# Three of the five sums of an entry's tile, formed over transposed blocks in PSUM instead of over rows in SBUF

## The chip, the cores and the metric

The kernel runs on one core of a Trainium2 chip. The metric is the device time in microseconds (us) of one execution, as the median over several runs. A profile of one execution gives the span (from the first instruction to the last), what each engine did, and what ended each wait. The engines are TensorE (PE, with its weight loads as PEld), VectorE (DVE), ScalarE (ACT) and GpSimd (POOL); SyncE (SP) issues nearly all of the transfers.

## The reference

A decoder block over 1024 tokens of width 1024, in fp32: a half-step FFN, a mixer of two branches with gates, a second half-step FFN and a last norm. What matters here is only its outline:

```python
def rms_norm(x, g):
    y = x * lax.rsqrt(jnp.mean(x * x, axis=-1, keepdims=True) + RMS_EPS)
    return y * g

def swiglu(x, w1, w3, w2):
    return (jax.nn.silu(x @ w1) * (x @ w3)) @ w2

h = x
h = h + 0.5 * swiglu(rms_norm(h, ffn1_norm), w1a, w3a, w2a)      # 1024 -> 2816 -> 1024
u = rms_norm(h, mix_norm)
proj = u @ w_in                        # 1024 -> 2304 (q, k, v) + 512 (pool) + 2048 (gates)
...                                    # dilated attention, multi-scale pooling
h = h + (sigmoid(gA) * yA + sigmoid(gB) * yB) @ w_out
h = h + 0.5 * swiglu(rms_norm(h, ffn2_norm), w1b, w3b, w2b)
out = rms_norm(h, final_norm)
```

So there are three places where normed rows enter a large product: the first FFN, the mixer's input projection and the second FFN. The document calls them the three *entries*.

## The kernel before, in words

**Products.** Each large product is done by blocks of a 2 x 2 split with seven products of half size instead of eight (`Sevens`, `Quad`). The right factor is the normed activation, transposed, so that its model columns lie on the partitions. Of its four blocks b11, b12, b21, b22 (first index: lower or upper half of the 1024 columns, `LOWS` and `HIGHS`; second index: lower or upper half of the 1024 tokens) seven right factors are formed:

- product 1: b11; product 2: b21; product 3: b22,
- product 5: t1 = b12 - b11; product 6: t2 = b22 - t1; product 4: t4 = t2 - b21; product 7: t3 = b22 - b12.

Each block is 512 columns by 512 tokens, and is held as a high and a low part (fp32r), because each step of a product takes three TensorE matmuls: high by high, high by low and low by high (L314). One call of `product` gives 128 output columns for 512 tokens: four steps of 128 in depth, three matmuls each, so 12 matmuls of 128 x 128 weights by 512 tokens. Products 1 and 2 add into one bank, and so do 5 and 3. A `Quad` holds the seven products of one group of columns, a `Pair` two such groups a and b (`u_f10a`, `u_f10b` in the profile: first FFN, pair 0).

**Left factors.** `Quad.operand(m)` forms the left factor of product m from weight blocks, with one sum on DVE for products 7 and 4 (L351 for 7) and two for product 6 (L345, L347), then `Sevens.split`: a copy to the high part on ACT (L303), and the difference as the low part (L306) on POOL, or on DVE for every third factor of a stage. Inside an entry `Entry.operand` names POOL for it. The factor tiles are `wc`, the block sums `s`.

**Rows to blocks.** The tokens come in eight tiles of 128 rows, t = 0 to 3 (the lower half) and t = 4 to 7 (the upper half). A tile is scaled by its norm on DVE (L267 for a whole row). `Rows` (L381 to L385) then makes a block's 128 tokens out of a row: four PE transposes of 128 x 128 into one bank of PSUM (L381), an ACT copy of the bank to the high part (L382), and, when `lower` is called, the low part by DVE (L385).

**An entry.** The lower tiles give b11 and b21, which are transposed ahead of the loop. The loop in `Entry.run` (L406 to L440) takes the upper tiles t = 4 to 7, with two products of other pairs per tile (i, and k = i + 1; all of them products 1 or 2, which need b11 and b21 alone) to keep PE busy while the sums and transposes of that tile are made. In a tile the order before is: product i; the transposes of b22; the sums t1, t2, t4 over rows on DVE (L423, L424, L425) and t3 over rows on POOL (L426); the lower of b22; the operand for i + 2; `out(i)`, which takes the finished product from PSUM; product k; the operand for k + 2; the transposes of t1, t2, t4, t3, sixteen of them; the scaling of the next row (`high(t + 1, 1)`, L267); four lowers on DVE; `out(k)`; `after(t)`, which squares a later row on ACT. t1 and t3 take the place of the lower tile's blocks in `h[t - 4]`, t2 and t4 a half tile `s` each. b12 itself is no factor of any product, so it is never transposed. `more` (L790) issues the operands of the first pair's products 6 and 7 as soon as tile 6 and tile 7 are through. These two, M6 and M7 below, are the first products behind the loop.

**Order.** Around the entries the order of the instructions on each engine is the order in which the program issues them (`tc.manual_schedule()`); each engine works its own queue in that order and waits at the head of it. Waits between engines follow from the tiles that they share: SBUF tiles by pool and tag, PSUM by whole banks (tag "acc" or "mm", a few banks each). Two operations on one bank from two engines are put one behind the other.

The first FFN's entry is written out in `begin_up1` (L792 to L893), with `rows(t, what, c)` scaling half a row and transposing it; the mixer's lower tiles are done by `rows_first` (L1232) inside the last steps of the first FFN's down product; those of the second FFN by `rows_first2` and `lower` (L1874 to L1882) beside the output projection.

## Time and profile before

| | |
|---|---|
| runs | 1957.8, 1959.87 and 1957.8 us; median 1957.8 us |
| profiled execution, span | 1955.6 us, 25018 instructions |
| PE busy | 1914.1 us, 98% of the span |
| DVE busy | 1343.5 us, 69% |
| ACT busy | 759.4 us, 39% |
| POOL busy | 741.1 us, 38% |
| mean granted TensorE clock | 0.994 |
| DMA | 333.57 MB, 171 GB/s mean |
| PE's largest groups | L706 (down products), three groups of 616 matmuls with 240.0 to 240.9 us each |

How to read it: a share of busy time is an average over all stages, so the entries have to be read by their own stretches: 28.16 to 59.78 us, 666.37 to 697.60 us and 1297.20 to 1328.90 us for the loops over the upper tiles, about 31 us each, 94.6 us in all. In rows of single instructions the first column is the start in us from the span's beginning, the second the time that the instruction (or the run of xN alike) took, then engine, line, operation, output<-inputs, sizes and type; brackets give the idle time before it and who ended it. A PE row "128*128 128x512" is a matmul with 128 x 128 weights and 512 columns.

### The profile page before, as it was taken

How to read it: one execution, taken by the hardware profiler on the slowest of the kernel's cores; microseconds unless marked ns; L12 is line 12 of the kernel's file. 1: busy time of each engine (PE TensorE's matmuls, PEld its weight loads, DVE VectorE, ACT ScalarE, POOL GpSimd, SP SyncE). 2: the span in 40 equal slices, each digit the busy share in tenths (PEclk: the TensorE clock that was granted, in tenths of full speed). 3: DMA queues.
4: the chain of work that ended last, by engine and by line, in shares of the span. 5: the costliest groups of instructions: out<-in, count | busy, mean ns of one | idle time of the engine just before them, and what ended most of it. 6: DMA issues, size and time to landing. Idle time of an engine off the chain costs nothing. (4 is left out here: it accounts for less than half of the span.)

```text
span 1955.6 us, 25018 instructions
## 1 busy us (share of the span) xinstructions
PE 1914.1 (98%) x8938; PEld 1579.7 (81%) x8938; DVE 1343.5 (69%) x2012; ACT 759.4 (39%) x1361; POOL 741.1 (38%) x557
## 2 busy tenths in 40 slices
PE   9999999999999999999998999999999999999997
PEld 7788888888888887888876878887788888878885
DVE  7776556557686876568774886887665556577766
ACT  6333333334344533334344662253333333333343
POOL 5333333332222444445454365543333333322231
PEclk9999999999999999999998999999999999999999
DMA  4155223336465546765658887643523223454653
GB/s 185 44 194 169 85 86 117 121 124 208 156 246 201 167 120 230 232 220 185 232 218 289 241 241 261 253 161 96 190 102 135 82 87 120 139 204 135 212 195 142
DMA packets 147005, 333.57 MB, mean 171 GB/s; under 512 B 20160, under 2 KB 40896, under 8 KB 145344
## 3 DMA queue, kind: packets, MB, share of 16 engines
q1 hardware_dynamic: 138096, 308.00, 45.9%
q10 hardware_dynamic: 8784, 23.96, 3.5%
q8 instruction: 71, 1.16, 0.2%
q14 instruction: 54, 0.44, 0.1%
HBM read 229.61 MB, written 102.30 MB: 170 GB/s over the span
## 5 line engine op out<-in xcount | busy, mean ns | idle before, releaser
L706 PE MATMUL d_f<-bhi_f,alo_f 128*128 128x512 f32 x616 | 240.8, 391 | 2.4 <-POOL alo_f L668 2.2
L706 PE MATMUL d_f<-bhi_f,ahi_f 128*128 128x512 f32 x616 | 240.9, 391 | 0.2 <-ACT ahi_f L664 0.2
L706 PE MATMUL d_f<-blo_f,ahi_f 128*128 128x512 f32 x616 | 240.0, 390 | 0.0
L668 POOL TENSOR_TENSOR alo_f<-g_f,ahi_f 128x512 fp32r<-128x512 f32 x70 | 99.2, 1434 | 298.5 <-ACT ahi_f L664 289.8
L314 PE MATMUL u_mixm<-xhi_t_mix,wc_mixm 128*128 128x512 f32 x608 | 196.0, 393 | 2.7 <-POOL wc_mixm L306 2.3
L314 PE MATMUL u_mixm<-xhi_b_mix,wc_mixm 128*128 128x512 f32 x456 | 149.3, 393 | 2.0 <-DVE y_m L982 2.0
L706 PEld LDWEIGHTS d_f<-bhi_f,alo_f 128*128 128x128 f32 x616 | 115.7, 188 | 29.0 <-POOL alo_f L668 4.0
L314 PEld LDWEIGHTS u_mixm<-xhi_t_mix,wc_mixm 128*128 128x128 f32 x608 | 113.8, 188 | 29.0 <-POOL wc_mixm L306 4.9
L706 PEld LDWEIGHTS d_f<-bhi_f,ahi_f 128*128 128x128 f32 x616 | 115.8, 188 | 24.1 <-ACT ahi_f L664 0.6
L706 PEld LDWEIGHTS d_f<-blo_f,ahi_f 128*128 128x128 f32 x616 | 115.8, 188 | 23.8
L314 PE MATMUL u_mixm<-xlo_t_mix,wc_mixm 128*128 128x512 f32 x304 | 118.6, 390 | 0.0
L306 POOL TENSOR_TENSOR wc_mixm<-s_mixm,wc_mixm 128x512 fp32r<-128x512 f32 x52 | 75.8, 1459 | 99.7 <-ACT wc_mixm L303 84.0
L314 PEld LDWEIGHTS u_mixm<-xhi_b_mix,wc_mixm 128*128 128x128 f32 x456 | 85.7, 188 | 20.7 <-ACT late_hi L1125 2.8
L303 ACT ACTIVATE wc_mixm<-s_mixm 128x512 fp32r<-128x512 f32 x76 | 47.6, 629 | 122.8 <-DVE s_mixm L347 52.1
L314 PE MATMUL u_mixm<-xlo_b_mix,wc_mixm 128*128 128x512 f32 x228 | 88.9, 390 | 0.0
L664 ACT ACTIVATE ahi_f<-g_f 128x1024 fp32r<-128x1024 f32 x84 | 81.8, 974 | 2.0 <-DMA g_f<-gs_f 2.0
L306 POOL TENSOR_TENSOR wc_mixm<-raw,wc_mixm 128x512 fp32r<-128x512 f32 x40 | 60.4, 1515 | 44.9 <-ACT wc_mixm L303 42.0
L664 ACT ACTIVATE bhi_f<-s_f2w 128x512 fp32r<-128x512 f32 x55 | 32.8, 627 | 97.1 <-DVE s_f2w L684 86.8
L1854 PE MATMUL wo<-w_o,o_hi 128*128 128x512 f32 x224 | 69.3, 391 | 0.0
L314 PEld LDWEIGHTS u_mixm<-xlo_t_mix,wc_mixm 128*128 128x128 f32 x304 | 57.2, 188 | 11.7 <-DVE xlo_t_mix L385 0.2
L664 ACT ACTIVATE bhi_f<-s_f1w 128x512 fp32r<-128x512 f32 x55 | 32.9, 630 | 85.1 <-DVE s_f1w L684 80.2
L1616 PE MATMUL yp<-pool_in,wab 128*128 128x512 f32 x192 | 55.7, 426 | 4.2 <-DMA pool_in<-pool 4.2
(1300 smaller groups left out, 5099.8 us busy)
## 6 DMA issues: line engine op xcount, KB each, us to landing
g_f<-gs_f SPq DMA_DIRECT2D x70, 512.0 KB, 4.5
gs_f<-y_f SPq DMA_DIRECT2D x88, 256.0 KB, 2.3
raw<-in_w2a_dram SPq DMA_DIRECT2D x35, 512.0 KB, 4.1
raw<-in_w2b_dram SPq DMA_DIRECT2D x35, 512.0 KB, 4.0
gs_f<-gb_f SPq DMA_DIRECT2D x46, 256.0 KB, 2.3
raw<-in_w1a_dram SPq DMA_DIRECT2D x22, 512.0 KB, 4.6
raw<-in_w3a_dram SPq DMA_DIRECT2D x22, 512.0 KB, 6.3
raw<-in_w1b_dram SPq DMA_DIRECT2D x22, 512.0 KB, 4.5
```

The source lines that it names most:

```text
L303: ac.activation(w[:, 0], src, AF.Copy)
L306: eng.tensor_tensor(w[:, 1], src, w[:, 0].bitcast(F32), op=OP.subtract)
L314: pe.matmul(p, a, b, start=(start and k == 0 and q == 0), stop=(k == 3 and q == 2), skip_group_check=not start)
L664: ac.activation(hi[:, c], src, AF.Copy)
L668: eng.tensor_tensor(lo[:, d], src[:, o], hi[:, d].bitcast(F32), op=OP.subtract)
L706: pe.matmul(self.banks[m][t], l, r, start=(first and q == 0), stop=(last and q == 2))
L1616: pe.matmul(p, a, b, start=(j == 0), stop=(j == 11))
L1854: pe.matmul(banks[m][t], l, r, start=(st == 0 and j == 0 and q == 0), stop=(st == 1 and j == 1 and q == 2))
```

## The change

In `Entry.run` three sums (t1, t2, t4) are formed from transposed blocks in PSUM, and only t3, the difference of a tile's own two blocks, is still formed over rows. Per upper tile, b22, b12 and t3 are transposed: 12 transposes instead of 20. The sums then read a transposed block in PSUM and a transposed block of the lower tile in SBUF, and write to PSUM:

- t1 = b12^T - b11^T, in b12's bank, in place;
- t2 = t3^T + b11^T, in a bank of its own (b22 - b12 + b11 is the same sum as b22 - t1);
- t4 = t2 - b21^T, in t2's bank, in place, once t2's parts are out.

For that, b11^T and b21^T of the lower tiles are kept: `Rows.keep` copies the bank of the transposes to the rows' own place in `h[t]` (ACT, eight copies of 128 x 512 per entry). A class `Parts` makes the high and the low part of such a sum, as `Rows` does without the transposes. t3 goes to a tile of its own and is issued on POOL at the head of a tile's work, ahead of product i. The order of a tile becomes: t3 (POOL); product i; transposes of b22, then b12; t1; transposes of t3; lower of b22; operand and output; product k; t2; lower of t1; operand; lower of t2; t4; lower of t3; the scaling of the next row; lower of t4; output.

In the first FFN, the b11 transposes of tile 3 go to a bank of the tag "mm" instead of "acc".

```diff
@@ class Rows
-            p = bank(tag, f"x_{what}_{t}")
+            p = self.flat = bank(tag, f"x_{what}_{t}")
...
+        def keep(self, dst):
+            ac.activation(dst.rearrange("p (k q) -> p k q", k=4), self.p, AF.Copy)
+
+    class Parts:
+        def __init__(self, X, what, src, t):
+            q = t % 4
+            self.hi, self.lo = (v[:, :, q * P:(q + 1) * P] for v in X[what])
+            self.src = src.rearrange("p (k q) -> p k q", k=4)
+            ac.activation(self.hi, self.src, AF.Copy)
+        def lower(self):
+            ve.tensor_tensor(self.lo, self.src, self.hi.bitcast(F32), op=OP.subtract)
@@ Entry.run
+                b11, b21 = (self.low[t - 4][:, c] for c in (LOWS, HIGHS))
+                t3 = self.sv.half_tile("s", f"t3_{t}")
+                gp.tensor_tensor(t3, y[:, HIGHS], y[:, LOWS], op=OP.subtract)
                 self.product(i)
                 if t + 1 < NT:
                     high(t + 1, 0)
-                lo = self.low[t - 4]
-                b11, b21, b12, b22 = lo[:, LOWS], lo[:, HIGHS], y[:, LOWS], y[:, HIGHS]
-                s = Rows(X, "b22", b22, t)
-                t1, t3 = b11, b21
-                t2, t4 = (self.sv.half_tile("s", f"{n}_{t}") for n in ("t2", "t4"))
-                ve.tensor_tensor(t1, b12, b11, op=OP.subtract)
-                ve.tensor_tensor(t2, b22, t1, op=OP.subtract)
-                ve.tensor_tensor(t4, t2, b21, op=OP.subtract)
-                gp.tensor_tensor(t3, b22, b12, op=OP.subtract)
+                s = Rows(X, "b22", y[:, HIGHS], t)
+                p12 = bank("acc", f"x_b12_{t}")
+                for j in range(4):
+                    c = slice(j * P, (j + 1) * P)
+                    pe.transpose(p12[:, c], y[:, c], ident)
+                ve.tensor_tensor(p12, p12, b11, op=OP.subtract)
+                r1 = Parts(X, "t1", p12, t)
+                r3 = Rows(X, "t3", t3, t)
                 s.lower()
                 self.operand(i + 2)
                 self.out(i)
                 self.product(k)
+                t2 = bank("acc", f"x_t2_{t}")
+                ve.tensor_tensor(t2, r3.flat, b11, op=OP.add)
+                r2 = Parts(X, "t2", t2, t)
+                r1.lower()
                 self.operand(k + 2)
-                rs = [Rows(X, what, src, t) for what, src in (("t1", t1), ("t2", t2), ("t4", t4), ("t3", t3))]
+                r2.lower()
+                ve.tensor_tensor(t2, t2, b21, op=OP.subtract)
+                r4 = Parts(X, "t4", t2, t)
+                r3.lower()
                 if t + 1 < NT:
                     y = high(t + 1, 1)
-                for r in rs:
-                    r.lower()
+                r4.lower()
                 self.out(k)
@@ begin_up1, rows_first, lower: the kept transposes, after the lowers
-        rows(3, "b11", LOWS)
+        rows(3, "b11", LOWS, "mm")
...
+        for t in range(4):
+            r[t].keep(h[t][:, LOWS])        # behind product 1's operand
...
+        for t in range(4):
+            r[t].keep(h[t][:, HIGHS])       # behind the last b21 lower
...
             for r in rs:
                 r.lower()
+            for r, c in zip(rs, (LOWS, HIGHS)):
+                r.keep(h[t][:, c])
```

More of the change, by code (lines that the diff above doesn't have):

```diff
@@ L814, in begin_up1, with rows @@
         r = {}
-        def rows(t, what, c):
+        def rows(t, what, c, tag="acc"):
             scaled_part(t, c, gain_row)
-            r[t] = Rows(X, what, h[t][:, c], t)
+            r[t] = Rows(X, what, h[t][:, c], t, tag)
         keep_on(12)
@@ L1878, in scaled2, with lower @@
         scaled(t, h[t] if t < 4 else rows_y[t], gain2)
-    def lower(rs):
+    def lower(t, rs):
         for r in rs:
             r.lower()
+        for r, c in zip(rs, (LOWS, HIGHS)):
+            r.keep(h[t][:, c])
     with tc.manual_schedule():
@@ L1947, in tile_block @@
         step_o(STEPS - 3, range(2))
-        lower(r[0])
-        lower(r[1])
+        lower(0, r[0])
+        lower(1, r[1])
         r.append(rows_first2(2))
         step_o(STEPS - 3, range(2, 4))
-        lower(r[2])
+        lower(2, r[2])
         r.append(rows_first2(3))
         adds_o(m - 1, range(2))
-        lower(r[3])
+        lower(3, r[3])
         adds_o(m - 1, range(2, 4))
```

## The prediction

> **What bounds the kernel now.** I read the page first, then the table by stretches for the three places that the change touches, then TensorE (PE), VectorE (DVE), ScalarE (ACT) and GpSimd (POOL) in order of time inside one of them.
>
> ```profile
> span 1955.6 us, 25018 instructions
> ...
> PE 1914.1 (98%) x8938; PEld 1579.7 (81%) x8938; DVE 1343.5 (69%) x2012; ACT 759.4 (39%) x1361; POOL 741.1 (38%) x557
> ```
>
> PE is busy 98% of the span, so the whole is bound by it. The three entries (first FFN, mixer, second FFN, four upper tiles each) are tighter. In the table by stretches the columns are the stretch, its length, then the busy time of PE, PEld, DVE, ACT and POOL; each stretch runs from the tile loop's first product to the first product behind the loop:
>
> ```profile
> 28.16:59.78 31.62, 31.25 (x178) 26.18 (x176) 27.77 (x37) 18.89 (x36) 20.91 (x15) 1.00 0.15 51
> 666.37:697.60 31.23, 30.88 (x178) 26.34 (x176) 27.21 (x38) 18.91 (x37) 19.58 (x14) 1.00 0.14 51
> 1297.20:1328.90 31.70, 31.06 (x178) 26.14 (x176) 28.22 (x40) 19.08 (x35) 17.41 (x12) 1.00 0.19 68
> ```
>
> PE fills 31.25 of 31.62 us, but DVE is close behind with 27.77: there is little room before DVE decides. One tile of the mixer's entry, first on PE, then on DVE:
>
> ```profile
> 676.78 0.60 PE L381 MATMUL x_b<-ident,hn_mix 128*128 128x128 f32 x4
> ...
> 680.41 1.04 PE L381 MATMUL x_t<-ident,s_mixt 128*128 128x128 f32 x8
> 681.29 0.60 PE L381 MATMUL x_t<-ident,h 128*128 128x128 f32 x4
> 684.47 0.60 PE L381 MATMUL x_b<-ident,hn_mix 128*128 128x128 f32 x4
> ...
> 678.68 1.94 DVE L267 SCALAR_TENSOR_TENSOR hn_mix<-h,nst,gain_mix 128x1024 f32<-128x1024 f32 x1
> 681.24 2.48 DVE L385 TENSOR_TENSOR xlo_t_mix<-x_t,xhi_t_mix 128x512 fp32r<-128x512 f32 x4 [0.63 <-ACT xhi_t_mix L382]
> ```
>
> A tile takes 684.47 - 676.78 = 7.69 us. Eight transposes take 681.29 - 680.41 = 0.88, four 0.44. DVE's next scaled row (call it y, L267) is ready at 680.62, almost 4 us before PE wants it for b22 at 684.47: PE never waits for y. Four lowers in a row take 2.48, so the pitch of DVE is (2.48 - 0.68) / 3 = 0.60.
>
> **The change, part by part.** *Removed:* 8 transposes per tile, 96 in all, 12 x 0.88 = 10.6 us of PE, the most that the change can give. A tile would then take PE 7.69 - 0.88 = 6.8.
>
> *Moved:* the three sums on DVE now read transposes, so they stand behind PE's transposes, and the next y stands behind them. DVE still issues eight 512-wide operations and the scaling, but y is now preceded by seven (sub, lower b22, t2, lower t1, lower t2, t4, lower t3) instead of four. ACT's queue counts too: t2's copy stands there behind those of t1, t3, the next operand and the product's output. Four copies in a row, first and last:
>
> ```profile
> 677.42 0.60 ACT L382 ACTIVATE xhi_b_mix<-x_b 128x512 fp32r<-128x512 f32 x1 [0.91 <-PE x_b L381]
> ...
> 678.91 0.63 ACT L303 ACTIVATE wc_mixm<-raw 128x512 fp32r<-128x512 f32 x1
> ```
>
> The pitch is 1.49 / 3 = 0.50. Let Y be the end of a tile's scaling, and 0.06 the step from an end to a start on another engine. PE starts b22 at Y + 0.06; b12's last result is there 0.44 + 0.60 later; sub starts at Y + 1.15 and ends at 1.83 (0.68). ACT takes up t1 at 1.89, t3 at 2.39, the operand at 2.89, the output at 3.39, t2 at 3.89, done at 4.49. T2's sum, held until t3's copy ends at 2.99 (the program lets two engines into one bank only in turn), is in time for that. DVE then waits for t2's copy, lowers t2 at 4.55, and does t4 at 5.15, lower t3 at 5.75 and the scaling at 6.35, which ends at Y + 7.62 if unhindered (1.27, the row at 1295.19 below). So a tile takes 7.62 where it took 7.69: PE's 0.88 becomes a wait for y, and three periods per entry win 0.2 us.
>
> *The last tile* loses. After tile 6, `more` issues operand 6 of the first pair, ahead of tile 7. In the first two entries its low part is POOL's, and in POOL's new order t3 of tile 7 still stands behind it; before, PE wanted t3 last of all, now ahead of the second product:
>
> ```profile
> 669.09 0.60 PE L381 MATMUL x_b<-ident,hn_mix 128*128 128x128 f32 x4
> ...
> 691.33 0.68 DVE L345 TENSOR_TENSOR s_mixm<-raw 128x512 f32<-128x512 f32 x1
> 692.05 0.69 DVE L347 TENSOR_TENSOR s_mixm<-s_mixm,raw 128x512 f32<-128x512 f32 x1
> 692.83 0.63 ACT L303 ACTIVATE wc_mixm<-s_mixm 128x512 fp32r<-128x512 f32 x1 [1.97 <-DVE s_mixm L347]
> 695.85 1.28 POOL L426 TENSOR_TENSOR h<-hn_mix 128x512 f32<-128x512 f32 x1 [0.63 <-DVE s_mixt L425]
> 697.18 0.66 PE L381 MATMUL x_t<-ident,h 128*128 128x128 f32 x4 [0.35 <-POOL h L426]
> 697.59 0.47 PE L314 MATMUL u_mixm<-xhi_t_mix,wc_mixm 128*128 128x512 f32 x1
> 699.11 0.68 DVE L351 TENSOR_TENSOR s_mixm<-raw,raw 128x512 f32<-128x512 f32 x1
> 701.93 0.73 PE L314 MATMUL u_mixm<-xhi_t_mix,wc_mixm 128*128 128x512 f32 x2 [0.63 <-POOL wc_mixm L306]
> ```
>
> After: lower t4 starts at Y - 0.08, L345 0.60 and L347 another 0.72 later, ending at Y + 1.93; ACT's copy ends at 2.65; POOL's low part runs to 3.98 and t3 to 5.26 (L426's 1.28 each). PE is through with b12 at Y + 0.93 and stands for 4.4 us until Y + 5.32. With b22 at 669.09 + 3 x 7.62 = 691.95, t3's transposes start at 697.2, the second product at 697.65, and the first product behind the loop (M6) at 700.4 instead of 697.59. DVE's chain goes on: t3's copy ends at 698.45, t2's sum at 699.2, its copy at 699.85, t4 at 701.2 (behind lower t2), its copy at 701.85; lower t4 from 701.9, L351 from 702.5 to 703.2, its copy to 703.9, its low part to 705.25. So the next product's (M7's) third matmul, the first that needs the low part, starts at 705.3 instead of 701.93: +3.4 us in the mixer.
>
> The other two entries, and what hides the rest:
>
> ```profile
> 24.88 0.63 ACT L303 ACTIVATE wc_f10a<-raw 128x512 fp32r<-128x512 f32 x1
> 28.16 0.39 PE L314 MATMUL u_f10a<-xhi_b_f,wc_f10a 128*128 128x512 f32 x1
> 30.88 0.60 PE L381 MATMUL x_b<-ident,x 128*128 128x128 f32 x4
> 54.34 0.60 PE L381 MATMUL x_b<-ident,x 128*128 128x128 f32 x4
> 64.71 0.74 PE L314 MATMUL u_f10a<-xhi_t_f,wc_f10a 128*128 128x512 f32 x2 [0.62 <-POOL wc_f10a L306]
> ...
> 627.80 1.17 ACT L664 ACTIVATE bhi_f<-s_f1w 128x512 fp32r<-128x512 f32 x2 [1.53 <-DVE s_f1w L684]
> ...
> 1281.41 1.26 PE L381 MATMUL x_b<-ident,h_again 128*128 128x128 f32 x8 [0.81 <-DVE xlo_b_f L385]
> 1295.19 1.27 DVE L267 SCALAR_TENSOR_TENSOR hn_f<-h_again,nst,gain_ffn 128x1024 f32<-128x1024 f32 x1
> 1299.77 0.60 PE L381 MATMUL x_b<-ident,hn_f 128*128 128x128 f32 x4
> 1309.23 1.28 ACT L477 ACT_TABLE_LOAD   x1
> 1323.43 0.60 PE L381 MATMUL x_b<-ident,hn_f 128*128 128x128 f32 x4
> 1333.79 0.74 PE L314 MATMUL u_f20a<-xhi_t_f,wc_f20a 128*128 128x512 f32 x2 [0.62 <-POOL wc_f20a L306]
> 1387.37 19.04 PE u_f22a L314 x84
> ```
>
> First FFN: four added copies (`keep`) stand ahead of the copy at 24.88 and push it to 26.88. POOL's low part then ends near 28.85; PE wants it at 28.16 + 0.45 and waits 0.25, so b22 of tile 4 moves from 30.88 to 31.13 and that of tile 7 comes at 31.13 + 22.86 = 54.0 (before 54.34). From there to M7's third matmul the mixer's working has 705.3 - 691.95 = 13.35; here one DVE output of 0.60 more stands ahead of L351: 67.95 instead of 64.71, +3.2.
>
> Second FFN: the table load of 1.28 now stands ahead of t2's copy in tile 5, so 3 x 7.62 + 1.28 = 24.15 us from tile 4 to tile 7 instead of 23.66, +0.5. M6's low part is DVE's here, so t3 is free; but L345 must wait for POOL's t3 (both read SBUF) and ends at Y + 1.9, L347 2.6, copy 3.3, low part 4.0, sub 4.65, t1's copy 5.3, t3's copy 5.8, t2's sum 6.55, copy 7.2, t4 8.55, copy 9.2, lower t4 and output 10.5, L351 11.2, copy 11.9, low part 13.2: M7's third matmul 13.2 after b22, before 1333.79 - 1323.43 = 10.36: +2.8. And the banks that PE waits for at 1281.41 now come free one ACT copy of 0.60 later, since `keep` waits for the lower: +0.6. In sum +3.9.
>
> The mixer's eight keeps lie in ACT's gaps in the down stage, the smallest of 1.53 us against two copies of 0.50: nothing; without that cover, 0.50 each. No DMA is added or moved. Behind M7, PE runs without a gap (84 matmuls in 19.04 us are the 2.72 per twelve of 28.16 to 30.88), so a delay stays: 3.2 + 3.4 + 3.9 = 10.5 us.
>
> A stall of 4.4 us also meets the clock. The trace has one place like it:
>
> ```profile
> 1128.00:1131.50 3.50, 1.44 (x11) 0.56 (x7) 2.19 (x5) 3.21 (x12) 2.71 (x3) 0.95 1.05 189
> 1131.50:1135.00 3.50, 3.50 (x11) 2.84 (x11) 3.12 (x12) 3.50 (x12) 2.90 (x3) 0.56 1.04 345
> ```
>
> PE was busy 1.44 of 3.5 us, and in the next 3.5 us the granted clock (third column from the end) was 0.56: a loss of 3.5 x 0.44 = 1.5 us. Behind the new stalls M6 would let M7's third matmul start at 700.4 + 2.72 + 0.45 = 703.6, 1.7 before its operand is there, and that covers most of the loss. I take +0.4 for each of the first two entries, with bounds 0 and 1.5. By the Trainium skill (TensorE: Matmul & The Clock Gate, Part 1: The HAM clock gate) the clock halves only after a whole idle window of some 3.4 us that runs free of the kernel. By that rule 4.4 us hold a whole window only for some phases, and the sum would be nearer to 10.5 than to 11.3.
>
> A DVE sum written to PSUM is not in this trace. Nearest is L385, which reads PSUM, with 0.68: taken. The lower end is the pitch 0.60, the upper a sum hindered by POOL as t2 was here:
>
> ```profile
> 25.59 1.68 POOL L306 TENSOR_TENSOR wc_f10a<-raw,wc_f10a 128x512 fp32r<-128x512 f32 x1 [1.82 <-ACT wc_f10a L303]
> ...
> 26.14 1.67 DVE L424 TENSOR_TENSOR s_f1t<-x,x 128x512 f32<-128x512 f32 x1
> ```
>
> Two of the sums (sub, t4) lie on the loop: at 1.67 a tile takes 2 us more, at 0.60 0.2 less. In sum 10.5 + 0.8 = 11.3 us on the profiled execution. Its span is 1955.6; the median of the runs, 1957.8, lies 2.2 above, which the change leaves. 1957.8 + 11.3 = 1969.
>
> **Rivals.** (1) *PE stays the bound and wins.* For it: PE is 98% busy and 10.6 us of its work go. It decides from the point where y follows the last y by 6.8 us or less: DVE must not wait for t2's copy, and in tile 7 t3 must not stand behind operand 6. Against it: both orders are fixed in the queues. Time 1957.8 - 10.6 = 1947. (2) *The loop is shorter, but the last tile stalls.* If DVE's wait for t2's copy (4.55 against 3.6 without it) vanishes, PE's 6.8 decides, and 9 periods win 0.8 each: 1969 - 7 = 1962. (3) *The clock falls in full in all three entries*, uncovered: 3 x 1.5 - 0.8 = 3.7 more, 1973. The row with 0.56 is for it, M7's wait against. (4) *Sums in PSUM are slow*, 1.18 (halfway from 0.68 to 1.67): 9 periods of 1.0 more, 1978. Only that no row excludes it speaks for it.
>
> **How the numbers follow.** A measurement of this kernel tells some 0.2%, 3.9 us, from no change: the bounds are 1953.9 and 1961.7. Forecast 0.57 (its own range 1965 to 1972), rival 1 0.06, rival 2 0.12, rival 3 0.18, rival 4 0.07. Faster is rival 1, 0.06; the same two thirds of rival 2, 0.08; slower all else, 0.86. The range from 1962 to 1976 leaves out rival 1, the better part of rival 2 and the upper part of rival 4, under 2 in 10.
>
> **What would show it.** Right: b22 transposes 7.5 to 7.8 us apart in tiles 4 to 7; DVE idle 0.6 to 1.1 before lower t2, ended by ACT; a PE gap of 4 to 5 us ahead of tile 7's t3 transposes in the first two entries, ended by POOL; a clock below 1.00 behind it; DVE's sums in PSUM at 0.65 to 0.75. Wrong: b22 near 6.8 apart (rivals 1, 2), no gap in tile 7 (rival 1), sums of 1 us (rival 4), or PE's waits further on shrinking, so that the delay is given back.

## The result, and the profile after

The changed kernel takes 1968.8 us (median of 1966.64 to 1971.36, four runs) where the kernel before, in the same comparison, takes 1958.1: ratio 1.005, 95% interval 1.0038 to 1.0062. It is slower by 10.7 us. The profiled execution has a span of 1967.3 us and took 1969.4.

From the page of the changed kernel, span and busy time (columns: busy us, share of the span, instructions):

```profile
span 1967.3 us, 24839 instructions
...
PE 1913.3 (97%) x8842; PEld 1572.9 (80%) x8842; DVE 1334.0 (68%) x2012; ACT 773.9 (39%) x1385; POOL 727.0 (37%) x557
```

PE issues 96 matmuls less, the transposes, but its busy time fell by 0.8 us only, not by 10.6. The mean granted clock of the whole span went from 0.994 to 0.990, and 0.4% of 1967 us are 7.9 us: by this estimate the lower clock made the remaining matmuls longer by most of what the 96 transposes had saved. ACT gained the kept copies (24 instructions, 14.5 us).

The table by stretches, each again from the tile loop's first product to the first product behind the loop:

```profile
28.49:65.57 37.08, 31.16 (x146) 24.17 (x144) 26.34 (x41) 20.12 (x38) 17.55 (x16) 0.91 0.14 43
671.85:708.03 36.18, 30.34 (x145) 23.69 (x144) 25.25 (x39) 19.41 (x38) 14.53 (x14) 0.95 0.12 44
1305.22:1339.82 34.60, 29.01 (x146) 22.32 (x144) 25.64 (x39) 19.57 (x35) 13.92 (x12) 1.00 0.25 80
```

Before, PE filled 31.25 of 31.62 us in the first FFN; now it stands for 5 to 6 us in each, in the first two entries at a granted clock of 0.91 and 0.95. Part of the longer stretches comes back directly behind them, so the loss is counted to product 7's third matmul, as in the prediction. (By its products' rows the second FFN's loop before goes from 1297.04 to 1328.86, 31.8 us, and not from 1297.20 to 1328.90.)

The mixer's entry in order of time, first PE, then DVE, then POOL:

```profile
690.14 0.63 PE L381 MATMUL x_b<-ident,hn_mix 128*128 128x128 f32 x4 [0.28 <-DVE hn_mix L267]
...
697.94 0.63 PE L381 MATMUL x_b<-ident,hn_mix 128*128 128x128 f32 x4 [0.36 <-DVE hn_mix L267]
698.40 0.60 PE L440 MATMUL x_b<-ident,hn_mix 128*128 128x128 f32 x4
703.33 1.12 PE L381 MATMUL x_t<-ident,s_mixt 128*128 128x128 f32 x4 [4.33 <-POOL s_mixt L432]
...
712.00 0.74 PE L314 MATMUL u_mixm<-xhi_t_mix,wc_mixm 128*128 128x512 f32 x2 [0.61 <-POOL wc_mixm L306]
...
691.24 0.70 DVE L441 TENSOR_TENSOR x_b<-x_b,h 128x512 f32<-128x512 f32 x1 [0.59 <-PE x_b L440]
...
693.09 0.70 DVE L449 TENSOR_TENSOR x_t<-x_t,h 128x512 f32<-128x512 f32 x1 [0.56 <-ACT xhi_t_mix L382]
...
694.58 0.69 DVE L401 TENSOR_TENSOR xlo_t_mix<-x_t,xhi_t_mix 128x512 fp32r<-128x512 f32 x1 [0.21 <-ACT xhi_t_mix L398]
695.31 0.70 DVE L454 TENSOR_TENSOR x_t<-x_t,h 128x512 f32<-128x512 f32 x1
...
696.51 1.28 DVE L267 SCALAR_TENSOR_TENSOR hn_mix<-h,nst,gain_mix 128x1024 f32<-128x1024 f32 x1
...
700.79 1.27 POOL L306 TENSOR_TENSOR wc_mixm<-s_mixm,wc_mixm 128x512 fp32r<-128x512 f32 x1 [4.35 <-ACT wc_mixm L303]
702.01 1.27 POOL L432 TENSOR_TENSOR s_mixt<-hn_mix 128x512 f32<-128x512 f32 x1
```

A tile takes 697.94 - 690.14 = 7.80 us (before 7.69), and PE waits for the scaled row (L267). A sum of DVE in PSUM takes 0.70. In tile 7 PE stands 4.33 us for t3, which POOL makes only after operand 6's low part. Product 7's third matmul comes at 712.00 instead of 701.93.

Two rows of PE show banks that come free late, behind a kept copy (L389), the first in the first FFN's down products, where the mixer's copies lie, the second ahead of the second FFN's entry (1.44 us, before 0.81):

```profile
643.57 0.50 PE L729 MATMUL d_f<-bhi_f,ahi_f 128*128 128x512 f32 x1 [0.46 <-ACT h L389]
...
1289.60 1.25 PE L381 MATMUL x_b<-ident,h_again 128*128 128x128 f32 x8 [1.44 <-ACT h_again L389]
```

Where the time went, by the start of the same PE instruction in both kernels. The last columns say how much more the changed kernel took in that part, in this pair of profiles and in a second pair (the runs "before again" and "after again" below):

| part, up to | before | after | pair 1 | pair 2 | forecast |
|---|---|---|---|---|---|
| first FFN's entry, product 7's third matmul | 64.71 | 69.46 | +4.75 | +4.30 | 3.2 + 0.4 |
| the mixer's first product | 666.37 | 671.85 | +0.73 | +0.54 | 0 |
| mixer's entry, product 7's third matmul | 701.93 | 712.00 | +4.59 | +4.52 | 3.4 + 0.4 |
| the first scores of the attention | 1056.94 | 1067.40 | +0.39 | +0.99 | 0 |
| the output projection's first product | 1201.40 | 1208.76 | -3.10 | -1.94 | 0 |
| the second FFN's first product | 1297.04 | 1305.22 | +0.82 | +0.50 | 0.6 |
| second FFN's entry, product 7's third matmul | 1333.79 | 1345.91 | +3.94 | +3.96 | 3.3 |
| the last down product | 1942.67 | 1954.35 | -0.44 | -2.58 | 0 |
| sum | | | +11.7 | +10.3 | 11.3 |

Of the first row 0.27 us in pair 1 and -0.53 us in pair 2 lie ahead of the entry's first product. Counted from that product the first FFN's entry takes 4.48 and 4.84 us more.

### The profile page after: what moved, and what is told of

Same layout as the page of the kernel before. It is cut to its first block, busy times and chain, and to the rows that moved or that the text cites. A ratio compares the mean times of both kernels' runs of the same rounds, so it can differ in the third digit from the quotient of the medians.

```text
span 1967.3 us, 24839 instructions
## 1 busy us (share of the span) xinstructions
PE 1913.3 (97%) x8842; PEld 1572.9 (80%) x8842; DVE 1334.0 (68%) x2012; ACT 773.9 (39%) x1385; POOL 727.0 (37%) x557
## 5 line engine op out<-in xcount | busy, mean ns | idle before, releaser
L314 PEld LDWEIGHTS u_mixm<-xlo_t_mix,wc_mixm 128*128 128x128 f32 x304 | 57.1, 188 | 11.7
```

The lines of the kernel that those rows point to most:

```text
L314: pe.matmul(p, a, b, start=(start and k == 0 and q == 0), stop=(k == 3 and q == 2), skip_group_check=not start)
```

## The experiments

The times of the kernel before, run beside them, have medians of 1959.46 (experiments 1 to 4), 1959.36 (5 to 7 and the first version of 8), 1956.98 (the second version of 8, and 9) and 1957.06 (10). Medians of different sets are compared by what each lies above the kernel before beside it; for the changed kernel that is 10.7 us in the first comparison (1958.1) and 10.4 us in "after again".

**1. t3 first.** In tile 7, t3 is issued on POOL ahead of operand 6.

```diff
+                if t < NT - 1:
                     t3 = ...            # tiles 4 to 6, as in the change
...
                 after(t)
+                if t == NT - 2:
+                    t3 = self.sv.half_tile("s", f"t3_{t + 1}")
+                    gp.tensor_tensor(t3, y[:, HIGHS], y[:, LOWS], op=OP.subtract)
                 if t >= NT - 2:
                     self.more(t - NT + 2)
```

> The changed kernel, but in tile 7 of each entry the difference t3 is issued on POOL ahead of the first pair's operand 6 (its sums, its copy and its low part), not behind it. My theory (tile 7 loses because t3 stands behind that low part on POOL): PE's gaps of 4.05 and 4.33 us ahead of tile 7's t3 transposes in the first two entries go, the granted clock stays at 1.00 behind them, and product 7's third matmul comes about 12.2 us behind tile 7's first b22 transpose instead of 14.4 (first FFN) and 11.5 instead of 14.1 (mixer); the second FFN stays at 13.2. In sum 4.7 us less than the changed kernel: 1964. Rival (tile 7 is bound by DVE's own chain, the gap on PE is only its shadow): less than 1 us, 1968.

Measured: 1965.49 us, ratio 1.0035 (1.0023 to 1.0048). The mixer's tile 7, PE in order of time:

```profile
695.91 0.63 PE L381 MATMUL x_b<-ident,hn_mix 128*128 128x128 f32 x4 [0.37 <-DVE hn_mix L267]
697.18 0.66 PE L381 MATMUL x_t<-ident,s_mixt 128*128 128x128 f32 x4 [0.20 <-POOL s_mixt L465]
...
707.79 0.73 PE L314 MATMUL u_mixm<-xhi_t_mix,wc_mixm 128*128 128x512 f32 x2
```

PE's wait for t3 is 0.20 instead of 4.33. Product 7's third matmul comes 707.79 - 695.91 = 11.88 us behind b22 (expected 11.5, changed kernel 14.06), in the first FFN 12.17 (12.2; 14.38), in the second FFN 13.17 as before it. By these distances the two entries win 2.2 us each, 4.4 together (expected 4.7). The median is 6.0 us above the kernel before, 4.4 to 4.7 less than the changed kernel's. So the order on POOL costs some 2 us in each of the first two entries, and the rival is out. What was not as expected: in the mixer the clock still fell, to 0.50 from 703.4 to 706.8, behind a wait of 1.70 us for t2's copy.

**2. DVE's order.** The row is scaled right behind t4, the lower of t4 is put off into the next tile. POOL as in the change.

```diff
                 s.lower()
+                if last:
+                    last.lower()
...
                 r4 = Parts(X, "t4", t2, t)
-                r3.lower()
                 if t + 1 < NT:
                     y = high(t + 1, 1)
-                r4.lower()
+                r3.lower()
+                last = r4
```

> The changed kernel with another order on DVE alone: the next row is scaled right behind t4, ahead of the lower of t3, and the lower of t4 is put off into the next tile, behind the lower of b22, where DVE waited for t3's copy. POOL's order stays. My theory (the tile's period of 7.80 us is the chain over DVE from one scaled row to the next): b22 transposes 6.8 to 7.1 us apart in tiles 4 to 7 instead of 7.8, in nine periods 6 to 8 us less: 1961 to 1963; the gaps of some 4 us in tile 7 stay. Rival (the period is set by ACT's queue or by sums that are slow in PSUM): 7.6 to 7.8 apart, 1968.

Measured: 1966.15 us, ratio 1.0042 (1.0027 to 1.0057); b22 transposes 7.44 to 7.58 us apart where no table load lies between. DVE and POOL in the mixer:

```profile
687.12 1.66 DVE L267 SCALAR_TENSOR_TENSOR hn_mix<-h,nst,gain_mix 128x1024 f32<-128x1024 f32 x1
...
686.40 1.29 POOL L306 TENSOR_TENSOR wc_mixm<-raw,wc_mixm 128x512 fp32r<-128x512 f32 x1 [0.20 <-ACT wc_mixm L303]
```

A miss: the median is 6.7 us above the kernel before, so 3.7 to 4.0 us are won instead of 6 to 8, and from an entry's first product to product 7's third matmul only 0.7, 0.8 and 0.8 us. One lower (0.60) less stood ahead of the scaling, but it now ran beside POOL's low part and took 1.66 us instead of 1.28, so the period fell by 0.3 only. And the scaling was still in the loop, behind t1, t2 and t4: moving lowers doesn't open that. By the Trainium skill (SBUF — State Buffer, SBUF: two separate sides) DVE with two inputs from SBUF and GpSimd share one pair of ports, and whoever starts first blocks the other for the whole instruction. The rows agree in direction: the low part ended 0.57 us after the scaling began, and the scaling took 0.38 longer. That is 0.2 us less than the whole overlap, which a block to the end would cost; the last section has more such pairs.

**3. Eight transposes put back.** They read the kept b11 and nobody reads them.

```diff
+            for n in range(8 if more is not None else 0):
+                pe.transpose(self.p[:, n % 4, :], more[:, n % 4 * P:(n % 4 + 1) * P], ident)
...
-                s = Rows(X, "b22", y[:, HIGHS], t)
+                s = Rows(X, "b22", y[:, HIGHS], t, more=b11)
```

> The changed kernel with the eight transposes per tile put back as work that nobody reads: eight transposes of the kept b11 ahead of those of b22, into the same bank. 96 more, 12 x 0.88 = 10.6 us of PE work. My theory (PE waits for the scaled row anyway): they fill that wait, 0 to 2 us in sum: 1969 to 1971. Rival (PE is the bound and the change's saving is real but given away elsewhere): 10.6 us more, 1979.

Measured: 1976.42 us (1974.02 to 1981.92), ratio 1.0093 (1.0075 to 1.0112), 17.0 us above the kernel before and so 6.3 to 6.6 above the changed kernel: between the two expectations. PE in the mixer:

```profile
683.36 1.04 PE L381 MATMUL x_b<-ident,h 128*128 128x128 f32 x8
684.67 0.60 PE L442 MATMUL x_b<-ident,hn_mix 128*128 128x128 f32 x4
691.55 1.04 PE L381 MATMUL x_b<-ident,h 128*128 128x128 f32 x8
```

Periods without the table load are 8.1 to 8.3 us instead of 7.80. What I had missed: PE's wait ahead of b22 is only some 0.5 us, so of the 0.88 us of added work 0.3 to 0.4 pushes the real transposes and the loop with them. From their first product to product 7's third matmul the three entries take 1.0, 1.8 and 1.1 us more than in the changed kernel's profile; the rest lies in stretches where nothing was added (see 6, 7 and 10). So the theory was wrong that PE has room for all eight, and the rival that it has room for none.

**4. Twelve transposes with the sums on rows.** The kernel before, without the transposes of t1 and t2.

```diff
-                rs = [Rows(X, what, src, t) for what, src in ...]
+                rs = [Parts(X, what, s.flat, t) if what in ("t1", "t2") else Rows(X, what, src, t)
+                      for what, src in ...]
```

> The kernel before with 12 transposes per tile and nothing else changed: the sums stay on rows, and the transposes of t1 and t2 are left out (their high and low parts are made from b22's bank, so t1 and t2 are not what the reference needs). My theory: PE's 7.69 us per tile fall to DVE's busy time of 27.77 / 4 = 6.94, so b22 transposes 6.9 to 7.1 apart, nine periods 6 us less: 1952, so that 12 transposes are worth something when DVE's sums don't wait for them. Rival (PE's transposes were hidden, or other waits take their place): 7.5 or more apart, 1957 to 1958.

Measured: 1953.52 us, ratio 0.9973 (0.9964 to 0.9982), 5.9 us faster than the kernel before. PE in the mixer:

```profile
668.85 0.60 PE L381 MATMUL x_b<-ident,hn_mix 128*128 128x128 f32 x4
...
675.70 0.60 PE L381 MATMUL x_b<-ident,hn_mix 128*128 128x128 f32 x4
...
681.22 0.73 PE L314 MATMUL u_mixm<-xhi_b_mix,wc_mixm 128*128 128x512 f32 x2 [0.81 <-POOL wc_mixm L306]
```

The first tile takes 6.85 us, which is PE's 7.69 less 0.84; the others 7.9 and 7.0, since PE then meets waits for operands on POOL. Up to the first product behind them the three loops are 1.0, 1.3 and 0.4 us shorter, but product 7 doesn't come earlier by as much: from an entry's first product to product 7's third matmul the profile has -0.2, -0.5 and +0.5 us against the kernel before, 0.2 us won in sum. The median came near what the theory had put (1952), but by luck: the gain lies in stretches that this version leaves as they were (144.5 us of attention and pooling before, 139.3 here; see 6, 7 and 10). In the entries other waits take the place of the transposes, as the rival has it. That fewer transposes can pay in the entries is shown by experiment 8 alone.

**5. PE kept busy in its gap.** 18 matmuls ahead of tile 7's t3 transposes in the first two entries, into the same bank.

```diff
+            x = X["b11"][0][:, 0, :]
+            for n in range(fill):
+                pe.matmul(p, x[:, :P], x, start=True, stop=True)
```

> The changed kernel, with 18 matmuls that nobody reads (128 rows by 512, 18 x 0.227 = 4.1 us) ahead of tile 7's t3 transposes in the first two entries, into the same bank: PE works through its gap of 4.05 and 4.33 us, all waits stay. What it tells is the clock's share. My theory: the granted clock stays at 1.00 behind tile 7, the four t3 transposes take 0.60 instead of 1.11 us, and product 7's third matmul comes 0.4 to 0.5 us earlier in each of the two: 1 us in sum, 1968. Rival (the clock costs in full, because nothing covers it): 1.5 or more each, 3 us, 1966.

Measured: 1967.38 us, ratio 1.0038 (1.0024 to 1.0053). The clock in the changed kernel around its three tiles 7, and in this run in the first FFN's (third column from the end):

```profile
54.50:57.90 3.40, 1.28 (x9) 0.86 (x8) 2.94 (x5) 0.94 (x2) 0.23 (x1) 1.00 0.45 147
57.90:61.30 3.40, 1.10 (x5) 1.10 (x6) 0.69 (x1) 0.66 (x2) 2.25 (x2) 0.51 0.02 7
61.30:64.70 3.40, 3.40 (x10) 2.63 (x9) 2.61 (x5) 1.68 (x3) 0.00 (x0) 0.50 0.00 0
...
703.10:706.50 3.40, 3.17 (x10) 2.69 (x11) 1.31 (x3) 1.68 (x3) 0.18 (x1) 0.50 0.00 0
...
1337.90:1341.30 3.40, 1.26 (x4) 0.86 (x5) 2.76 (x5) 1.63 (x5) 0.00 (x0) 1.00 0.01 4
1341.40:1344.70 3.30, 3.30 (x9) 2.37 (x8) 2.30 (x4) 1.29 (x3) 0.13 (x1) 0.50 0.00 0
```

```profile
58.00:61.40 3.40, 3.40 (x17) 2.57 (x17) 0.61 (x2) 1.00 (x3) 1.75 (x2) 1.00 0.00 0
```

With the filling the clock stays at 1.00, and product 7's third matmul comes 13.98 and 13.65 us behind b22 instead of 14.38 and 14.06: 0.4 us in each, as the theory had it. The clock's full price doesn't arrive, because product 7 waits for its operand in any case. The median is 2.4 us below that of the changed kernel beside it (1969.76). Of that the two entries explain 0.8, so the distances decide between theory and rival, not the median.

**6 and 7. Both kernels again**, for the stretch of attention and pooling, which the change does not touch.

> The kernel before once more, for the stretch from the first product of the attention's scores to the output projection's first product, which the change does not touch: 144.8 us in the profile before, 141.7 in that of the changed kernel, 139.6 to 144.0 in four experiments. My theory: it differs by some 5 us between executions of any kernel here, so this profile shows anything from 139 to 145. Rival: the change gives back 3 us there, and this profile shows 144 to 145 again.

> The changed kernel once more, for the same stretch. My theory: anything from 139 to 145 us there, while product 7's third matmuls come as before (14.4, 14.1 and 13.2 us behind tile 7's first b22 transpose), within 0.3 us. Rival: 141 to 142 again.

Measured: 1959.42 us (ratio to the kernel before 1.0, 0.999 to 1.0009) and 1969.76 (1.0052, 1.0035 to 1.007). Product 7's third matmul comes 14.71, 14.07 and 12.16 us behind tile 7's first b22 transpose, where 14.4, 14.1 and 13.2 within 0.3 were expected: right in the mixer, just outside in the first FFN, 1.0 off in the second FFN. There the transpose itself came late, 8.83 us behind that of tile 6, behind a stretch of halved clock (1328.5 to 1331.9); from the entry's first product to product 7's third matmul both profiles have 40.7 us. The attention's stretch in the kernel before again, in the changed kernel's first profile and in the run with the filling:

```profile
1057.48:1202.46 144.98, 134.26 (x916) 112.22 (x915) 109.85 (x377) 82.96 (x267) 53.52 (x47) 0.95 0.81 244
```

```profile
1067.40:1208.76 141.36, 134.60 (x916) 112.77 (x915) 109.95 (x377) 82.97 (x267) 53.58 (x47) 0.94 0.83 246
```

```profile
1066.47:1204.44 137.97, 131.56 (x915) 110.69 (x915) 109.94 (x378) 83.02 (x267) 53.56 (x47) 0.98 0.83 252
```

The work is the same (DVE 109.9, ACT 83.0, POOL 53.5 us), the length is not: 1.7 us apart between two executions of the changed kernel (141.4 and 143.0), and 138.0 with the filling. But both profiles of the kernel before have the longest stretch of all, 144.5 and 145.0. So my theory, any value from 139 to 145 for any kernel, is not borne out for that kernel, and the rival (141 to 142 again) not for the changed one. The second untouched stretch, from the second FFN's product 7 to the last down product, goes the same way: 608.9 and 610.4 before, 608.4 and 607.8 after.

The traces show where the spread of the attention's stretch sits. Over the fourteen profiles its first 60 matmuls take 15.3 to 18.3 us and its 421st to 480th 8.8 to 13.3 us; the other groups of 60 agree within 0.2 us, but for the second (7.9 to 9.6). At both places PE's wait goes back to a transfer. In the kernel before, PE, then ACT and POOL:

```profile
1069.78 1.22 PE L1616 MATMUL yp<-pool_in,wab 128*128 128x512 f32 x2 [2.50 <-DMA pool_in<-pool]
...
1130.11 0.71 PE L1526 MATMUL tp<-ident,e 128*128 128x128 f32 x2 [1.85 <-ACT e L1506]
...
1128.29 0.63 ACT L1374 ACTIVATE w_o<-w_o_in 128x512 fp32r<-128x512 f32 x1 [5.34 <-POOL w_o_in L1371]
...
1126.97 2.51 POOL L1371 TENSOR_TENSOR w_o_in<-w_o_in,w_o_in 128x512 f32<-128x512 f32 x2 [6.88 <-DMA w_o_in<-in_w_o_dram]
```

ACT's row for `e` stands behind its copy of `w_o`, that behind POOL's sum, and that waits for a load. Where POOL waits 6.0 to 7.4 us for that load (eleven profiles), PE waits 0.95 to 2.37 us, in step with POOL, and the group takes 10.5 to 13.3 us; where POOL waits 4.2 to 4.6 us (the changed kernel's first profile, experiments 4 and 5), PE doesn't wait, and it takes 8.8 to 9.1. So the spread comes from when transfers land, and from the clock that is halved behind some of these waits. Why they land earlier or later, and whether the change has a part in it, is open.

**8. The scaling out of the loop** (two versions). The sums and the 12 transposes stay; the first version moves the scaling right behind the lower of b22:

```diff
...
                 s.lower()
+                if t + 1 < NT:
+                    y = high(t + 1, 1)
+                else:
+                    self.more(0)
                 self.operand(i + 2)
...
                 r2 = Parts(X, "t2", t2, t)
-                r1.lower()
-                self.operand(k + 2)
-                r2.lower()
+                if t + 1 < NT:
+                    r1.lower()
+                    self.operand(k + 2)
+                    after(t)
+                    t3 = third(t + 1)
+                    r3.lower()
+                    r2.lower()
+                else:
+                    self.more(1)
+                    r2.lower()
+                    r3.lower()
                 ve.tensor_tensor(t2, t2, b21, op=OP.subtract)
                 r4 = Parts(X, "t4", t2, t)
-                r3.lower()
-                if t + 1 < NT:
-                    y = high(t + 1, 1)
-                r4.lower()
+                if t == NT - 1:
+                    r1.lower()
                 self.out(k)
+                r4.lower()
...
```

`third` is t3 on POOL, for the next tile. `keep` of the first FFN's b21 comes behind operand 5 and output 3, that of the second FFN's blocks directly behind their transposes.

> The changed kernel's sums with other orders. DVE: the next row is scaled right behind the lower of b22, so it no longer stands behind t2 and t4; then t2, lower t1, lower t3, lower t2, t4, output, lower t4. POOL: t3 of the next tile ahead of whatever follows, so ahead of operand 6. Tile 7: the sums of operand 6 where the scaling stood, that of operand 7 right behind t2. The kept copies of the first FFN's b21 come behind the operands, those of the second FFN ahead of its lowers. My theory (the 7.80 us are a loop: scaled row, transposes, t1, t2, t4, next scaled row): with the scaling out of that loop a tile takes PE's 6.8 us or DVE's 6.9 to 7.1; nine periods win 6 to 8 us against the kernel before, tile 7 about nothing, the mixer's kept copies still lose 0.5: 1951 to 1953 where the kernel before has 1958 to 1959. Rival (DVE's work is the limit whatever its order): 7.5 or more apart, 1957 or above.

Measured: 1948.75 us, ratio 0.9951 (0.9938 to 0.9964). PE and DVE in the mixer:

```profile
674.46 0.60 PE L381 MATMUL x_b<-ident,hn_mix 128*128 128x128 f32 x4
...
681.75 0.60 PE L381 MATMUL x_b<-ident,hn_mix 128*128 128x128 f32 x4
...
681.81 0.69 DVE L401 TENSOR_TENSOR xlo_t_mix<-x_t,xhi_t_mix 128x512 fp32r<-128x512 f32 x1 [0.66 <-ACT xhi_t_mix L398]
```

The periods (7.23 to 7.34 us without the table load) are between theory and rival: PE no longer waits for the scaled row, but DVE waits 0.66 us for t4's copy. Product 7's third matmul comes 9.26 us behind b22 in the first two entries (before: 10.37 and 9.77), but 11.61 in the second FFN (10.36). The median is 10.6 us below that of the kernel before, more than expected; by the profile the entries, from their first product to product 7's third matmul, give 4.7 of it against "before again" (2.7, 1.9 and 0.1), and most of the rest is in the two untouched stretches of 10. The second version fills the wait and has three moves more:

```diff
+                self.operand(i + 2)
                 s = Rows(X, "b22", y[:, HIGHS], t)
...
-                self.operand(i + 2)
-                self.out(i)
+                if t + 1 < NT:
+                    self.out(i)
                 self.product(k)
...
                 if t + 1 < NT:
-                    r1.lower()
                     self.operand(k + 2)
...
                 else:
+                    self.out(i)
                     self.more(1)
...
-                if t == NT - 1:
-                    r1.lower()
+                r1.lower()
                 self.out(k)
...
-                     lambda n: first.A.operand((6, 7)[n]))
+                     lambda n: first.A.operand((6, 7)[n], gp))
```

> The version with the scaling out of the loop (b22 transposes 7.25 us apart there, bound by DVE's 0.66 us wait for t4's copy and by PE's wait for a low part on POOL), with four more moves: the operand for i + 2 ahead of the transposes; the lower of t1 put off behind t4, so that it fills the wait for t4's copy; in tile 7 the output of product i behind t2; and the low parts of operands 6 and 7 on POOL in all entries. My theory: PE's own 6.76 us of work decide in the mixer and the second FFN, 6.8 to 6.9 apart, 6.9 to 7.1 in the first FFN; nine periods win 3 us more, the second FFN's operand 6 another 1: 1944 to 1946 where the kernel before has 1958 to 1959. Rival (another chain of the same length stands behind, such as the squares and the inverse norm): 7.2 or more apart, 1948 to 1949.

Measured: 1943.0 us, ratio 0.9934 (0.9921 to 0.9948), 14 us faster than the kernel before beside it (1956.98). The mixer's stretch from the loop's first product to the first one behind it:

```profile
663.99:692.97 28.98, 28.02 (x145) 22.84 (x144) 24.63 (x37) 18.48 (x36) 13.59 (x14) 1.00 0.16 55
```

28.98 us where the kernel before has 31.23, PE busy for 28.02 of them: PE is the bound again, with less work. From their first product to product 7's third matmul the three entries win 3.3, 2.6 and 3.7 us, 9.7 of the 14; most of the rest is again in the two untouched stretches. The first period is 6.8 us in each entry, as expected, the others 7.1 to 7.5, as the rival has them. In these PE waits 0.15 to 0.51 us for t3, which stands on POOL directly behind a low part:

```profile
682.00 0.66 PE L381 MATMUL x_t<-ident,s_mixt 128*128 128x128 f32 x4 [0.26 <-POOL s_mixt L428]
...
679.40 1.30 POOL L306 TENSOR_TENSOR wc_mixm<-raw,wc_mixm 128x512 fp32r<-128x512 f32 x1 [2.97 <-issue]
680.66 1.29 POOL L428 TENSOR_TENSOR s_mixt<-hn_mix 128x512 f32<-128x512 f32 x1
```

The scaling takes 1.32 to 1.86 us in these six tiles, again beside POOL's low part, but no b22 transpose waits for it.

**9. No kept copies in the mixer.**

```diff
             for r in rs:
                 r.lower()
-            for r, c in zip(rs, (LOWS, HIGHS)):
-                r.keep(h[t][:, c])
```

> The changed kernel without the mixer's eight kept copies (its sums then read rows where they need transposes, so t1, t2 and t4 of the mixer are not what the reference needs). My theory: the stretch of the first FFN from product 7's third matmul to the mixer's first product is 602.4 us with them and 601.7 without (before: 601.7), so that they cost 0.6 to 0.7 us, of which PE's wait on a bank at 643.57 is 0.46. Rival (something else in that stretch moved): 602.4 without them too.

Measured: one execution, 1967.56 us. The stretch from product 7's third matmul in the first FFN to the mixer's first product, without the copies, in the changed kernel, and in the kernel before:

```profile
69.68:671.30 601.62, 600.32 (x2670) 496.18 (x2671) 402.83 (x536) 215.39 (x333) 191.84 (x148) 1.00 0.44 153
```

```profile
69.46:671.85 602.39, 600.50 (x2671) 496.04 (x2671) 402.20 (x536) 220.22 (x341) 190.94 (x148) 1.00 0.45 153
```

```profile
64.71:666.37 601.66, 600.38 (x2671) 496.54 (x2671) 402.97 (x537) 215.28 (x333) 190.71 (x148) 1.00 0.45 153
```

601.6 against 602.4, the kernel before 601.7, and PE's wait at 643.57 is gone: the mixer's copies cost 0.7 us. The other profiles agree: the four without these copies (the kernel before twice, experiment 4 and this one) have 601.6 to 601.8 us here, the ten with them 602.0 to 602.5.

**10. PE's instructions at the start.** The two untouched stretches together took 753.3, 755.4 and 754.0 us in the three profiles of kernels with 20 transposes per tile (before, before again, experiment 3, where 8 of the 20 are added work), and 746.5 to 751.0 in the nine with 12. What divides them might be the mere number of PE's instructions. 96 matmuls more, at the start, in the changed kernel and in the second version of 8:

```diff
-        keep_on(12)
+        keep_on(108)
```

> The changed kernel with 96 more matmuls of 128 x 128 that nobody reads, at the very start, where PE only keeps its clock up while the first rows are loaded: as many PE instructions as the kernel before has. Two stretches that the change doesn't touch (from the first scores to the output projection's first product, and from the second FFN's product 7 to the last down product) take 753.3 and 755.4 us together in the two profiles of the kernel before and 754.0 with eight transposes put back (8938 matmuls each), and 746.5 to 751.0 in nine profiles with 8842 or 8878. Theory A (the number of PE's instructions ahead of them decides, whatever they do): 753 or more here too. Theory B (chance, or what the transposes do in their place): 746 to 751. The start itself costs what PE's added matmuls take there, 5 to 11 us.

> The same 96 matmuls at the start of the second version with the scaling out of the loop (749.3 us in the two stretches): a second look at the same question. Theory A: 753 or more. Theory B: 746 to 751.

Measured: 1992.89 and 1967.28 us. The start grew by 20 us, twice what I had expected, since the profile has 192 matmuls more and not 96 (9034 in all). The medians rose by 24 to 25 us, the profiled executions by 19 and 22; what goes beyond the start is not explained. The two stretches took 749.1 and 751.5 us together, the second 0.5 above theory B's range, both below theory A's 753. So the number of PE's instructions is not it. Whether eight transposes more in their place have an effect so far behind them, or three high values out of 14 came by chance, is open.

## Why the prediction was right, and where it was not

Forecast 1969, measured 1968.8 in the first comparison and 1969.8 in the second. The direction and the mechanism were right; the sum was right in part by luck, since terms that were 3 us too small met 3 to 4 us given back elsewhere.

- *The loop (7.62 us forecast): right in kind, 0.18 too short.* PE's saving turned into a wait for the scaled row, as told. The lower of t2 starts 4.59 us behind the end of the scaling (694.58 - 689.99; forecast 4.55). DVE's idle time is split, 0.56 ahead of t2's sum and 0.21 ahead of the lower of t2, where I had 0.6 to 1.1 ahead of the latter alone. The step that was mis-sized is t4's place: it starts 695.31 - 694.58 = 0.73 behind the lower of t2 and not the pitch of 0.60. Three periods were to take 22.86 us. In the mixer they take 23.37 (697.94 - 674.57), 0.3 more than before where 0.2 was to be won; in the first FFN 23.44, as before (23.46) where 0.6 was to be won; in the second FFN, with the table load in tile 5, 24.8 us (1332.74 - 1307.95) instead of the forecast 24.15.
- *DVE's sums in PSUM: 0.70*, where 0.68 was taken. Rival 4 is out, and rival 2 with it: the loop got no shorter.
- *Tile 7 in the first two entries: right.* The wait of 4.33 and 4.05 us for POOL (forecast 4.4); experiment 1 removes it by the order on POOL alone. From b22 to product 7's third matmul the second FFN has 13.17 (forecast 13.2), the first FFN 14.38 (13.95 + 0.4), the mixer 14.06, 0.3 more than 13.35 + 0.4.
- *The clock: +0.4 in each of the first two, right* (experiment 5), although it fell in all three entries, as rival 3 had it. What rival 3 had wrong is that nothing would cover it: product 7 waits for its operand anyway.
- *The mixer's kept copies, costed at nothing: wrong.* I looked for gaps on ACT, and there were gaps; but the copy holds a PSUM bank longer, and PE waited for that bank. 0.7 us (experiment 9). For the second FFN I had counted just that, with 0.6; there it cost 0.8 and 0.5.
- *The sum: near by chance or by something unexplained.* The entries and the kept copies cost 14.8 us in pair 1 (4.75 + 0.73 + 4.59 + 0.82 + 3.94) and 13.8 in pair 2 (14.6 and 14.3 from the first FFN's first product on), not 11.3. Stretches that the change doesn't touch gave 3.2 and 3.5 back, which no step of mine had. The traces of 6 and 7 put the largest of them down to when transfers land, and experiment 10 excludes PE's number of instructions; whether the change has a part in it stays open.
- *Rival 1, that PE's saving arrives,* did not happen. It had two conditions: the next row must not wait for t2's copy, and t3 of tile 7 must not stand behind operand 6. Experiment 1 meets the second alone, and its entries still lose 8.6 us; the first version of experiment 8 meets both, with other moves, and its entries win 4.7; the second version's win 9.7, with the same sums and transposes, at 1943.0 us. What the first condition is worth alone was not run.

## What to carry to other kernels

Before an operation is moved to the far side of another engine's work, look at what stands behind it in its own queue: here a scaling that had been four microseconds early became the last link of a loop, and orders on DVE, ACT and POOL decided between 13 us lost and 9.7 us won in the three entries with the same transposes. A copy that is hidden on its engine may still not be free: ask for how long it holds its bank, and who wants that bank next. And when a forecast hits, add it up by stretches all the same: two terms were too small here, and stretches outside the change made up for them. In experiment 4 such a stretch gave nearly the whole gain, and the median alone would have confirmed a wrong theory.

## What the runs showed of the hardware that was not expected

- The clock was halved behind slices in which PE had not stood still throughout: behind 54.50 to 57.90 with 1.28 us busy, mostly transposes, and behind 1337.90 to 1341.30 with 1.26 us, all of them products (rows in experiment 5). By the Trainium skill (TensorE: Matmul & The Clock Gate, Part 1: The HAM clock gate) it falls after an idle window of some 3.4 us; here a window that was busy for more than a third was enough, while in the mixer PE did stand still through the whole slice ahead (699.7 to 703.1). The halved stretches in the entries are 3.4 or 6.8 us long, which agrees with its window. In each trace all halved stretches begin whole multiples of 3.41 us apart. Cut into slices at these points, the fourteen traces have 31 slices at full clock with PE busy (by the profile) for less than 46% of them, and a halved slice follows each; from 46 to 67% it follows 22 of 75, and above 67% none of 7763. A halved clock came back only behind slices that were busy for 91% or more.
- A scaling of 1.28 us took 1.32 to 2.32 when it began beside a low part on POOL. In all 17 such scalings of experiment 2 and of the second version of 8 the loss is 0.2 us less than the overlap: 0.05 for 0.24 us, 0.38 for 0.57, 0.54 for 0.73, 1.04 for 1.24. Where a row is to be ready early, POOL's queue has to be looked at too.
- One and the same stretch of attention and pooling took between 138.0 and 145.0 us in the profiles of kernels that do the same work there, at a granted clock between 0.94 and 0.98.
